# Batched norms in the query and key path of a two-layer hybrid block: copy out of PSUM by ScalarE, one reciprocal root per product

## The chip, the core and the metric

The kernel runs on one core of one Trainium2 chip. The metric is device time in microseconds (us) of one execution. Before the change it is 1564.75 us, the median of three runs (1563.94 to 1565.75). The trace comes from one further profiled execution, which took 1565.54 us; its instructions span 1563.8 us.

The engines are named as in the profile: PE (TensorE, matrix products and transposes), PEld (its weight loads), DVE (VectorE), ACT (ScalarE), POOL (GpSimd), SP (SyncE, which issues the DMAs). Each engine runs its own instructions strictly in order; they wait for each other by semaphores.

## The reference, cut to what matters

```python
for l in range(2):                                  # 512 latent tokens, 256 context tokens, width 1024
    h  = modulate(rms_norm(x,  g_mix[l]), sh1, sc1)
    hc = modulate(rms_norm(xc, g_mix[l]), csh1, csc1)
    aq, ak, av, bu, bv, cin, dq, dk, dv = split_cols(h @ w_in[l])     # and the same of hc
    # (in the last layer only keys and values are taken of hc)
    q_a = axial_rope(rms_norm(heads(aq, 4), a_q_gain[l]), rows, cols) # heads of 64
    k_a = axial_rope(rms_norm(heads(ak, 2), a_k_gain[l]), rows, cols)
    out_a = window_attention(q_a, k_a, ...)                           # + context keys + sink
    out_d = neighbourhood_attention(rms_norm(heads(dq, 4), d_q_gain[l]),
                                    rms_norm(heads(dk, 4), d_k_gain[l]), ...)
    out_b = spatial_gating(bu, bv, ...);  out_c = multiscale_pool(cin, ...)
    x = x + g1 * (concat(out_a, out_b, out_c, out_d) @ w_out[l])
    x = x + g2 * swiglu(modulate(rms_norm(x, g_ffn[l]), sh2, sc2), ...)
    # layer 0: the context tokens go the same way, with dense attention among themselves
```

What the change touches is `rms_norm(heads(...))`: every query and key head of 64 numbers is scaled by `1 / sqrt(mean(q*q) + 1e-6)`, one root per token and head.

## The kernel before

All products are float32, split into a high and a low part; one product is three matmuls (`mm3`, lines 65, 66 and 67). Tokens of the input projection lie in three tiles of 256, called 4 (the context), 0 and 2 (`tiles`, line 550). `tok_proj` (line 535) makes one tile's product in one PSUM bank: two halves of 128 tokens, eight slices of the width, three matmuls each, 48 matmuls of 256 columns.

`post_qk` (line 473) follows each such product. ACT squares the bank into an SBUF tile (L479), DVE sums each head's squares (L481), ten small DVE instructions take the reciprocal root (`rsqrt`, L100 to L109), DVE multiplies the bank by it (L484), so the bank is free after L484. Then come the gain (L486), for window attention the rotation (L495 to L498), up to four PE transposes into the one "tq" bank (L510), and the splits of that bank into high and low parts for the scores: ACT L525, L531, L532, DVE L526, L533. The next tile's transposes need that bank empty.

There are 23 such calls. In layer 0: `d_proj(0)` three, `d_proj(1)` three, `a_proj` three for keys and three for queries. In layer 1: `d_ctx` two on one bank, each `d_proj` two, `a_proj` three and two.

Neighbourhood attention of a pair of heads is `d_group`: four blocks of 128 queries (`d_pair`, line 615), in layer 0 two context blocks more (`ctx_pair`). A block does for each of its two heads: scores (PE L367, L368, four matmuls into an "sc" bank), two DVE instructions that add the bias and take the running minimum into an SBUF tile "T" (L628, L630), the exponential (ACT L359, with a row of its own for the sum), the reciprocal (DVE L361) and the scaling (DVE L362). Then PE transposes T (L337), ACT copies the transposes (L344), PE multiplies them by the values (L349, into "po"), and ACT copies that out (L354). Window attention (`a_group`) is alike.

The stages of a layer, in the order of the program: pools and values, `d_proj(0)`, `d_group(0)`, `d_proj(1)`, in layer 0 `mod_unit` (which makes modulation vectors: matmuls L154, transposes L143), `d_group(1)`, `a_proj`, `a_group(0)`, `b_proj`, `a_group(1)`; then the output projection and the feed-forward part.

That order is not the order on the engines. The framework plays the whole program through when it builds it and lets each engine take what is ready first, so products of a later stage are put between the matmuls of an attention block. What holds this back are the rings of tiles: a tag has a fixed number of buffers, handed out in the order of the program, and the user of a buffer waits for the last reader of the one before.

```python
BUFS = {"h": 8, "x": 8, "st": 8, "w": 6, "raw": 3, "mraw": 2, "T": 3, "pts": 3, "bias": 2, "row": 3, "post": 4,
        "br": 1}                                          # SBUF rings, lines 31 and 32
BANKS = {"pj": 2, "sc": 2, "tq": 1, "pt": 1, "po": 1, "md": 1}   # PSUM banks, line 33
```

So there are two "pj" banks for products, one "tq" bank, three "T" tiles, which attention alone uses, and four "post" tiles, which `post_qk` and `b_proj` use. The bias tiles of a `d_pair` (ring "bias") are made by POOL (L612).

Of the kernel before, what the change touches and what calls it, by code (L numbers as in the profile page):

```python
# [27 lines left out]
EPS = 1e-6  # L28
# [11 lines left out]
def hybrid_block(ctx: ExitStack, tc, t, out):  # L40
# [53 lines left out]

    def rsqrt(src, n, scale, eps):

        x = small.tile([128, 8], F32, tag="rx", name="rx")[:, :n]
        y = small.tile([128, 8], F32, tag="ry", name="ry")[:, :n]
        z = small.tile([128, 8], F32, tag="rz", name="rz")[:, :n]
        V.tensor_scalar(x, src, scale, eps, op0=OP.mult, op1=OP.add)  # L100
        V.tensor_scalar(y.bitcast(I32), x.bitcast(I32), -0.5, MAGIC, op0=OP.mult, op1=OP.add)
        V.tensor_mul(z, y, y)
        V.scalar_tensor_tensor(z, z, -0.5, x, op0=OP.mult, op1=OP.mult)
        V.scalar_tensor_tensor(y, z, 1.5, y, op0=OP.add, op1=OP.mult)
        V.tensor_mul(z, y, y)
        V.tensor_mul(z, z, x)
        V.tensor_scalar(x, z, 0.375, -1.25, op0=OP.mult, op1=OP.add)
        V.tensor_mul(z, z, x)
        V.scalar_tensor_tensor(y, z, 1.875, y, op0=OP.add, op1=OP.mult)  # L109
        return y  # L110
# [274 lines left out]
    for l in range(DEPTH):  # L385
# [84 lines left out]

        grid = "p (r b c) -> p b r c"

        def post_qk(ps, b, nq, nk, gain, ng, rope, Q, K, window, c0=0):

            nh = nq + nk
            p3 = ps.rearrange("p (i x) -> p i x", i=2)[:, :, c0:c0 + 64 * nh].rearrange("p i (h d) -> p i h d", d=64)
            flat = "p i h d -> p (i h) d"
            s2 = tile("post", [128, 2, nh, 64])
            S.activation(s2, p3, AF.Square)  # L479
            ss = small.tile([128, 8], F32, tag="ss", name="ss")  # L480
            V.tensor_reduce(ss[:, :2 * nh], s2.rearrange(flat), axis=AX.X, op=OP.add)  # L481
            r = rsqrt(ss[:, :2 * nh], 2 * nh, 1.0 / 64, EPS).rearrange("p (i h) -> p i h", i=2)
            n_ = tile("post", [128, 2, nh, 64])
            V.tensor_tensor(n_, p3, r.unsqueeze(3).to_broadcast([128, 2, nh, 64]), op=OP.mult)  # L484
            if ng:
                V.tensor_tensor(n_[:, :, 0:ng], n_[:, :, 0:ng],  # L486
                                gain.unsqueeze(1).unsqueeze(1).to_broadcast([128, 2, ng, 64]), op=OP.mult)
            if rope:
                rot = tile("post", [128, 2, nh, 64])
                for i in range(2):  # L490
                    nv = n_[:, i].rearrange("p h (x f c) -> p h x f c", x=2, f=2)
                    rv = rot[:, i].rearrange("p h (x f c) -> p h x f c", x=2, f=2)
                    sv = sinT[:, b + i].rearrange("p (x f c) -> p x f c", x=2, f=2)
                    for f in range(2):
                        V.tensor_tensor(rv[:, :, :, f], nv[:, :, :, 1 - f],  # L495
                                        sv[:, :, f].unsqueeze(1).to_broadcast([128, nh, 2, 16]), op=OP.mult)
                V.tensor_tensor(n_, n_, cosT[:, b:b + 2].unsqueeze(2).to_broadcast([128, 2, nh, 64]), op=OP.mult)
                V.tensor_add(n_, n_, rot)  # L498
            t0 = 128 * b

            w = window and b < 4
            pt = psum("tq")
            for j in range(nh // 2):
                for i in range(2):
                    dst = pt[:, 256 * j:256 * j + 256]
                    if w and 2 * j < nq:
                        dst = dst.rearrange("p (w i r c) -> p i r w c", w=4, i=2, r=2)[:, i]
                    else:
                        dst = dst[:, 128 * i:128 * i + 128]
                    T.transpose(dst, n_[:, i, 2 * j:2 * j + 2], ident)  # L510
            halves = [slice(64 * e, 64 * e + 64) for e in range(2)]
            for j in range(nh // 2):
                src = pt[:, 256 * j:256 * j + 256]
                if 2 * j < nq:

                    for e in range(2):
                        own, other = [Q[j][halves[x], e] for x in (e, 1 - e)]
                        if w:
                            own, other = [x[:, :SEQ].rearrange("p (w y x) -> p w y x", w=4, y=2)[:, :, b // 2]
                                          for x in (own, other)]  # L520
                            y = src[halves[e]].rearrange("p (w x) -> p w x", w=4)
                        else:
                            own, other = [x[:, t0:t0 + 256] for x in (own, other)]
                            y = src[halves[e]]
                        S.activation(own, y, AF.Copy)  # L525
# [33 lines left out]
        def d_ctx():  # L559

            w = wsplit(t["win_dk"][0], eng=G) + wsplit(t["win_dk"][1], eng=G)
            Ks = []
            ps = tok_proj(w, 4, 0, 256)
            for p in range(2):
                Ks.append(d_keys())
                post_qk(ps, 4, 0, 2, gd, 0, False, None, Ks[p], True, 128 * p)
            return Ks

        def d_proj(p, K=None):
# [1 line left out]
            bs = (0, 2) if K else tiles  # L571
            K = K or d_keys()
            Q = tile("st", [128, 2, NT], F32R)
            for bi, b in enumerate(bs):
                ps = tok_proj(w, b, 0, 256, [["pj", "sc", "pj"], ["pj", "pj", "pj"]][p][bi])
                post_qk(ps, b, 2, 2, gd, 2, False, [Q], K, True)
            return Q, K

        def d_values(pss, tag):
# [94 lines left out]
        def a_proj():  # L674
# [2 lines left out]
            K = d_keys()  # L677
            VA = tile("row", [128, 6, 128])
            w = group_units("win_a", 1)
            for b in tiles:  # L680
                ps = tok_proj(w, b, 0, 256)
                S.activation(VA[:, b:b + 2], ps.rearrange("p (i x) -> p i x", i=2)[:, :, 128:256], AF.Copy)
                post_qk(ps, b, 0, 2, gak, 2, b < 4, None, K, False)
            Q = [tile("st", [128, 2, NT], F32R) for _ in range(2)]
            w = group_units("win_a", 0)
            for b in tiles:
                if last and b == 4:
                    continue
                ps = tok_proj(w, b, 0, 256)
                post_qk(ps, b, 4, 0, gaq, 4, b < 4, Q, None, False)  # L690
            return Q, K, VA, amask


# [394 lines left out]
```

## Time and profile before

| what | value |
|---|---|
| median of three runs | 1564.75 us |
| the profiled execution | 1565.54 us, of which its instructions span 1563.8 us |
| PE | 1518.4 us busy, 97% of the span |
| DVE | 963.7 us, 62% |
| ACT | 618.1 us, 40% |
| POOL | 122.2 us, 8% |
| DMA | 104 GB/s in the mean |

How to read it: PE is the engine that is busy nearly throughout, so a microsecond counts when it makes PE stand still or makes its instructions longer. "Idle before, releaser" names the instruction whose end ended a wait. The ends of matmuls are modelled (a row of 0.28 us is followed by the next after 0.12 us), so what a matmul costs is read from the starts of successive rows. PEclk is the granted clock of TensorE, 1.00 at its upper level of 2.4 GHz; a stretch in which part of the time is at the lower level of 1.2 GHz shows a number between 0.5 and 1.

### The profile page before, as it was taken

To read this page: it belongs to the slowest core of one execution; us is meant where nothing else is said; L and a number is where in the kernel's file an instruction comes from. 1 tells how busy PE (TensorE), PEld (TensorE's weight loads), DVE (VectorE), ACT (ScalarE), POOL (GpSimd) and SP (SyncE) were. 2 spreads that over 40 slices of the span, in tenths; PEclk is the share of its full clock that TensorE was granted. 3 is DMA by queue.
4 is the path that set the end of the run, shared out by engine and by line. 5 is a ranking of instruction groups with operands and counts; after the bars stand their busy time and mean duration, and the time that the engine had idled before them with its cause. 6 is when DMAs were issued, how large, how long until landed. Compare 5 with 4: busy or idle time off the path is not lost.

```text
span 1563.8 us, 26196 instructions
## 1 busy us (share of the span) xinstructions
PE 1518.4 (97%) x10098; PEld 1336.1 (85%) x10098; DVE 963.7 (62%) x2335; ACT 618.1 (40%) x1276; POOL 122.2 (8%) x107
## 2 busy tenths in 40 slices
PE   7889999999999999999999998899999999999999
PEld 4668888788888888888888887788889998998997
DVE  4797876686485624833384467789856543454453
ACT  5546655643322112221222354457654332332331
POOL 2431000000000000000000005632000000000000
PEclk9899999999999999999999999999999999999999
DMA  8433133342243313622272231111223333223323
GB/s 309 122 115 116 48 110 129 122 139 75 88 142 113 117 62 115 222 59 64 93 248 59 78 113 55 58 55 47 81 82 102 95 84 105 90 87 102 95 82 100
DMA packets 79325, 163.39 MB, mean 104 GB/s; under 512 B 12001, under 2 KB 17761, under 8 KB 79201
## 3 DMA queue, kind: packets, MB, share of 16 engines
q1 hardware_dynamic: 79200, 161.73, 32.8%
q8 instruction: 79, 1.29, 0.3%
q14 instruction: 46, 0.37, 0.1%
HBM read 157.50 MB, written 4.19 MB: 103 GB/s over the span
## 4 chain that ended last, share of the span: by engine, by line
PE 89%; DVE 5%; ACT 1%; issue 0%; DVEq 0%; ACTq 0%
PE pj L65 9%; PE pj L66 9%; PE pj L67 9%; PE sc L66 6%; PE sc L65 6%; PE sc L67 6%; PE tq L65 3%; PE po L349 3%; PE tq L66 3%; PE tq L67 3%; PE po L65 3%; PE po L66 3%; PE po L67 3%; PE pt L66 2%; PE pt L67 2%; PE pt L65 2%
## 5 line engine op out<-in xcount | busy, mean ns | idle before, releaser
L82 ACT ACTIVATE w<-raw 128x512 fp32r<-128x512 f32 x368 | 227.5, 621 | 640.1 <-PE sc L67 159.5
L83 DVE TENSOR_TENSOR w<-raw,w 128x512 fp32r<-128x512 f32 x336 | 227.3, 679 | 244.7 <-ACT w L82 244.2
L65 PE MATMUL pj<-w,h 128*128 128x256 f32 x480 | 141.5, 295 | 12.8 <-DVE post L484 6.7
L66 PE MATMUL pj<-w,h 128*128 128x256 f32 x480 | 140.0, 292 | 2.9 <-DVE w L83 2.9
L67 PE MATMUL pj<-w,h 128*128 128x256 f32 x480 | 139.4, 291 | 0.0
L65 PE MATMUL pj<-st,w 128*128 128x258 f32 (+2 forms) x384 | 120.6, 314 | 2.5 <-ACT st L253 2.3
L66 PE MATMUL pj<-st,w 128*128 128x258 f32 (+2 forms) x384 | 120.4, 314 | 0.7 <-DVE st L254 0.7
L66 PE MATMUL sc<-st,w 128*128 128x258 f32 (+2 forms) x384 | 120.0, 313 | 0.0
L65 PE MATMUL sc<-st,w 128*128 128x258 f32 (+2 forms) x384 | 119.9, 312 | 0.0
L67 PE MATMUL pj<-st,w 128*128 128x258 f32 (+2 forms) x384 | 119.8, 313 | 0.0
L67 PE MATMUL sc<-st,w 128*128 128x258 f32 (+2 forms) x384 | 119.2, 311 | 0.0
L65 PEld LDWEIGHTS pj<-w,h 128*128 128x128 f32 x480 | 94.4, 197 | 21.1 <-issue 9.3
L83 POOL TENSOR_TENSOR w<-raw,w 128x512 fp32r<-128x512 f32 x32 | 44.2, 1398 | 742.2 <-ACT w L82 721.7
L66 PEld LDWEIGHTS pj<-w,h 128*128 128x128 f32 x480 | 94.7, 197 | 4.4 <-DVE w L83 3.1
L67 PEld LDWEIGHTS pj<-w,h 128*128 128x128 f32 x480 | 94.3, 197 | 1.3 <-issue 1.2
L65 PEld LDWEIGHTS pj<-st,w 128*128 128x128 f32 x384 | 73.1, 191 | 9.5 <-ACT st L253 3.5
L66 PEld LDWEIGHTS pj<-st,w 128*128 128x128 f32 x384 | 72.8, 190 | 5.7 <-DVE st L254 0.9
L67 PEld LDWEIGHTS pj<-st,w 128*128 128x128 f32 x384 | 72.7, 190 | 5.7 <-issue 1.7
L65 PEld LDWEIGHTS sc<-st,w 128*128 128x128 f32 x384 | 73.2, 191 | 4.6
L66 PEld LDWEIGHTS sc<-st,w 128*128 128x128 f32 x384 | 72.8, 189 | 4.4
L67 PEld LDWEIGHTS sc<-st,w 128*128 128x128 f32 x384 | 72.4, 189 | 4.2
L65 PE MATMUL po<-st,w 128*128 128x512 f32 (+1 forms) x192 | 66.5, 346 | 0.0
(304 smaller groups left out, 4125.8 us busy)
## 6 DMA issues: line engine op xcount, KB each, us to landing
mraw<-in_wmod SPq DMA_DIRECT2D x80, 512.0 KB, 3.7
raw<-in_wg SPq DMA_DIRECT2D x88, 256.0 KB, 2.6
raw<-in_wu SPq DMA_DIRECT2D x88, 256.0 KB, 2.6
raw<-in_wd SPq DMA_DIRECT2D x64, 256.0 KB, 2.7
h<-in_wslab SPq DMA_DIRECT2D x16, 512.0 KB, 7.8
raw<-in_wout SPq DMA_DIRECT2D x32, 256.0 KB, 2.6
x<-in_xt SPq DMA_DIRECT2D x16, 384.0 KB, 5.8
raw<-in_wd SPq DMA_DIRECT2D x32, 192.0 KB, 2.4
```

What stands on the lines that cost most here:

```text
L65: T.matmul(ps, ah, bh, start=start, stop=False)
L66: T.matmul(ps, ah, bl, start=False, stop=False)
L67: T.matmul(ps, al, bh, start=False, stop=stop)
L82: S.activation(w[:, 0, :n], raw, AF.Copy)
L83: eng.tensor_sub(w[:, 1, :n], raw, w[:, 0, :n].bitcast(F32))
L349: T.matmul(o[64 * hh:64 * hh + 64, :128], vs[hh][lo:hi], pts[i, hh], start=i == 0, stop=i == n - 1)
```

## The change

`post_qk` is cut in two. `qk_take` copies the bank to a "post" tile on ACT (new L477), squares the bank on ACT into a tile of ring "T" (L479), and lets DVE sum the squares (L480). `qk_takes` does this for all token tiles of a product, into one 24-column tile, and then calls `rsqrt` once. `qk_give` multiplies the SBUF copy by the roots (L493), then gain (L495), rotation (whose second tile is now in ring "T" too), transposes (L519) and splits (ACT L534, L540, L541; DVE L535, L542). `rsqrt` is called 9 times rather than 23 times. `d_ctx` squares and sums its bank once.

```diff
-        def post_qk(ps, b, nq, nk, gain, ng, rope, Q, K, window, c0=0):
+        def qk_take(ps, nh, ss):
+            p3 = ps.rearrange("p (i x) -> p i x", i=2)[:, :, :64 * nh].rearrange("p i (h d) -> p i h d", d=64)
+            n_ = tile("post", [128, 2, nh, 64])
+            S.activation(n_, p3, AF.Copy)
+            s2 = tile("T", [128, 2, nh, 64])
+            S.activation(s2, p3, AF.Square)
+            V.tensor_reduce(ss, s2.rearrange("p i h d -> p (i h) d"), axis=AX.X, op=OP.add)
+            return n_
+
+        def qk_takes(n, nh, pss):
+            ss = small.tile([128, 24], F32, tag="ss", name="ss")[:, :2 * nh * n]
+            ns = [qk_take(next(pss), nh, ss[:, 2 * nh * j:2 * nh * j + 2 * nh]) for j in range(n)]
+            r = rsqrt(ss, 2 * nh * n, 1.0 / 64, EPS).rearrange("p (n i h) -> p n i h", i=2, h=nh)
+            return [(x, r[:, j]) for j, x in enumerate(ns)]
+
+        def qk_give(n_, r, b, nq, nk, gain, ng, rope, Q, K, window):
             nh = nq + nk
-            s2 = tile("post", [128, 2, nh, 64])
-            S.activation(s2, p3, AF.Square)
-            ss = small.tile([128, 8], F32, tag="ss", name="ss")
-            V.tensor_reduce(ss[:, :2 * nh], s2.rearrange(flat), axis=AX.X, op=OP.add)
-            r = rsqrt(ss[:, :2 * nh], 2 * nh, 1.0 / 64, EPS).rearrange("p (i h) -> p i h", i=2)
-            n_ = tile("post", [128, 2, nh, 64])
-            V.tensor_tensor(n_, p3, r.unsqueeze(3).to_broadcast([128, 2, nh, 64]), op=OP.mult)
+            V.tensor_tensor(n_, n_, r.unsqueeze(3).to_broadcast([128, 2, nh, 64]), op=OP.mult)
...
             if rope:
-                rot = tile("post", [128, 2, nh, 64])
+                rot = tile("T", [128, 2, nh, 64])
...
         def d_proj(p, K=None):
...
-            for bi, b in enumerate(bs):
-                ps = tok_proj(w, b, 0, 256, [["pj", "sc", "pj"], ["pj", "pj", "pj"]][p][bi])
-                post_qk(ps, b, 2, 2, gd, 2, False, [Q], K, True)
+            tags = ["pj", "pj" if p else "sc", "pj"]
+            for b, x in zip(bs, qk_takes(len(bs), 4, (tok_proj(w, b, 0, 256, tags[i]) for i, b in enumerate(bs)))):
+                qk_give(*x, b, 2, 2, gd, 2, False, [Q], K, True)
```

What this does to the order of the instructions is shown at three places.

On PE in layer 0, about the transposes of `d_proj(0)`; before, with the products of its third tile (pj_1524) and the modulation's L154 about those of its second tile:

```order
L67 MATMUL pj_1440<-w_1432,h_692 128x256
L154 MATMUL md_1692<-mraw_1695,cact_79 32x512 x2
L154 MATMUL md_1692<-mraw_1701,cact_79 32x512 x2
L510 MATMUL tq_1007<-ident_75,post_1004 128x2x4x16 x2
L510 MATMUL tq_1007<-ident_75,post_1004 128x128 x2
L154 MATMUL md_1692<-mraw_1703,cact_79 32x512 x2
L154 MATMUL md_1692<-mraw_1709,cact_79 32x512 x2
L65 MATMUL pj_1524<-w_1417,h_635 128x256
```

After the change, at the same place (pj_1470 is the second product of `d_proj(1)`, sc_1116 the first scores of `d_group(0)`):

```order
L67 MATMUL pj_1470<-w_1407,h_692 128x256
L154 MATMUL md_1642<-mraw_1651,cact_79 32x512 x2
L519 MATMUL tq_1032<-ident_75,post_904 128x128 x4
L154 MATMUL md_1642<-mraw_1653,cact_79 32x512 x2
L154 MATMUL md_1642<-mraw_1659,cact_79 32x512 x2
L154 MATMUL md_1642<-mraw_1661,cact_79 32x512 x2
L519 MATMUL tq_1049<-ident_75,post_958 128x2x4x16 x2
L519 MATMUL tq_1049<-ident_75,post_958 128x128 x2
L154 MATMUL md_1642<-mraw_1667,cact_79 32x512 x2
L154 MATMUL md_1642<-mraw_1669,cact_79 32x512 x2
L143 MATMUL md_1677<-ident_75,mraw_1675 128x128 x4
L519 MATMUL tq_1066<-ident_75,post_1012 128x2x4x16 x2
```

The three tiles' transposes, which had products between them, follow one another with only L154 and L143 between; the products have moved ahead of all three.

On ACT in layer 0, in `d_group(0)`; before, at its first exponentials (post_1657 takes the squares of the second product of `d_proj(1)`, pj_1608):

```order
L359 ACTIVATE T_1146,sum_1150<-T_1146,m1_1147 128x448
L82 ACTIVATE w_2048<-raw_2046 128x512
L82 ACTIVATE w_2306<-raw_2304 128x512
L479 ACTIVATE post_1657<-pj_1608 128x512
L157 ACTIVATE mraw_1725<-md_1692 128x512
L82 ACTIVATE w_2311<-raw_2309 128x512
L525 ACTIVATE st_1439<-tq_1509 64x256
L359 ACTIVATE T_1160,sum_1164<-T_1160,m1_1161 128x448
```

After, at the last exponentials of the same group (L668, those of the second context block); pj_1416 and pj_1470 are the first two products of `d_proj(1)`, which were copied out by L477 ahead of the group's first exponential:

```order
L668 ACTIVATE T_1369,sum2_1370<-sc_1360,mn_1366 128x256
L668 ACTIVATE T_1369,sum2_1370<-sc_1361,mn_1366 128x256
L344 ACTIVATE pts_1314<-pt_1313 128x384
L344 ACTIVATE pts_1314<-pt_1313 64x128
L479 ACTIVATE T_1467<-pj_1416 128x512
L354 ACTIVATE x_1103<-po_1304 128x8x16
L479 ACTIVATE T_1521<-pj_1470 128x512
L344 ACTIVATE pts_1349<-pt_1348 128x512
```

The squares of the next product, which stood between the exponentials, stand behind the last of them.

On PE in layer 1, in `d_group(1)`; before, a stretch of a block (pj_11140 is a product of `a_proj`, sc scores, pt transposes, po the product with the values):

```order
L65 MATMUL pj_11140<-w_11033,h_9606 128x256
L367 MATMUL sc_10607<-st_9878,st_10355 128x256
L368 MATMUL sc_10607<-st_9875,st_10355 128x256
L337 MATMUL pt_10566<-ident_75,T_10542 128x128 x2
L337 MATMUL pt_10566<-ident_75,T_10542 64x128
L66 MATMUL pj_11140<-w_11033,h_9606 128x256
L349 MATMUL po_10309<-pts_10311,row_9744 64x128
L67 MATMUL pj_11140<-w_11033,h_9606 128x256
L349 MATMUL po_10309<-pts_10319,row_9744 64x128
```

After, the same group at its first block:

```order
L337 MATMUL pt_10425<-ident_75,T_10401 128x128 x2
L337 MATMUL pt_10425<-ident_75,T_10401 64x128
L337 MATMUL pt_10425<-ident_75,T_10401 128x128
L367 MATMUL sc_10504<-st_9701,st_10226 128x256
L368 MATMUL sc_10504<-st_9698,st_10226 128x256
L337 MATMUL md_10434<-ident_75,T_10415 128x128 x2
L337 MATMUL md_10434<-ident_75,T_10415 64x128
L337 MATMUL md_10434<-ident_75,T_10415 128x128
L349 MATMUL po_10424<-pts_10426,row_9663 64x128
L367 MATMUL sc_10518<-st_9701,st_10226 128x256
```

No product stands in the group any more until its last block; the group's own transposes, scores and value products follow each other.

## Rows read from the trace of the kernel before

**Rows 1.** The page's busy times, share of the span and instructions of each engine.

```profile
PE 1518.4 (97%) x10098; PEld 1336.1 (85%) x10098; DVE 963.7 (62%) x2335; ACT 618.1 (40%) x1276; POOL 122.2 (8%) x107
```

**Rows 2.** Busy time by stretches: PE, PEld, DVE, ACT, POOL, clock, DMA share, GB/s.

```profile
70.00:115.00 45.00, 38.16 (x268) 32.63 (x266) 42.87 (x102) 24.25 (x50) 18.51 (x15) 0.94 0.32 100
115.00:310.00 195.00, 194.32 (x1565) 162.59 (x1564) 145.69 (x510) 116.09 (x287) 12.86 (x16) 1.00 0.33 107
...
975.00:1026.00 51.00, 40.17 (x294) 38.75 (x294) 41.73 (x98) 20.49 (x44) 30.30 (x28) 0.92 0.21 65
1026.00:1165.00 139.00, 139.00 (x1099) 121.99 (x1098) 111.50 (x373) 91.19 (x222) 18.32 (x16) 1.00 0.19 60
```

**Rows 3.** Waits of PE: us in total, times, longest.

```profile
PE tq L510 <- DVE st L533: 6.7, 2, 3.5
PE pj L65 <- DVE post L484: 6.7, 3, 3.5
```

**Rows 4.** Timeline of ACT and DVE: first and last split of a tile.

```profile
121.28 0.38 ACT L525 ACTIVATE st<-tq 64x256 fp32r<-64x256 f32 x1 [3.96 <-PE tq L510]
...
125.15 0.43 DVE L533 TENSOR_TENSOR st<-tq,st 64x256 fp32r<-64x256 f32 x1 [0.15 <-ACT st L532]
```

**Rows 5.** Lines view, 70 to 310 us, L154: count, busy us, mean ns.

```profile
L154 PE MATMUL md<-mraw,cact 128*32 128x512 f32 x96 | 21.1, 638 | 0.0
```

**Rows 6.** Timeline of PE in layer 1: start, duration, instruction, idle time before.

```profile
997.49 0.38 PE L65 MATMUL pj<-w,h 128*128 128x256 f32 x1 [2.52 <-DVE post L484]
997.72 0.28 PE L66 MATMUL pj<-w,h 128*128 128x256 f32 x1
997.83 0.28 PE L67 MATMUL pj<-w,h 128*128 128x256 f32 x1
...
1003.57 0.52 PE L65 MATMUL pj<-w,h 128*128 128x256 f32 x1 [3.55 <-DVE post L484]
...
1004.11 0.41 PE L67 MATMUL pj<-w,h 128*128 128x256 f32 x1
1004.32 0.41 PE L65 MATMUL pj<-w,h 128*128 128x256 f32 x1
```

**Rows 7.** Lines view by form, 1040 to 1090 us: attention of layer 1.

```profile
L630 DVE TENSOR_SCALAR_CACHE_REDUCE T<-sc,m 128x256 f32<-128x256 f32 x14 | 6.7, 477 | 0.1
L362 DVE TENSOR_SCALAR T<-T,rs 128x512 f32<-128x512 f32 x8 | 6.1, 767 | 0.0
L359 ACT ACTIVATE T<-T,m 128x512 f32<-128x512 f32 x8 | 5.8, 719 | 3.0 <-DVE T L630 2.0 <-DVE rz L103 0.9
...
L628 DVE CUSTOM_DVE_ANT_0 T<-sc,bias 128x256 f32<-128x256 f32 x8 | 3.3, 415 | 0.0
...
L361 DVE RECIPROCAL rs<-sum 128x1 f32<-128x1 f32 x14 | 2.2, 157 | 0.4 <-ACT T L359 0.3
```

**Rows 8.** The same view, 80 to 310 us: layer 0.

```profile
L362 DVE TENSOR_SCALAR T<-T,rs 128x512 f32<-128x512 f32 x16 | 7.8, 485 | 0.1
```

**Rows 9.** Timeline of PE: value products of two successive blocks of layer 1.

```profile
1054.24 1.09 PE L349 MATMUL po<-pts,row 128*64 128x128 f32 x14
1055.26 0.66 PE L337 MATMUL md<-ident,T 128*128 128x128 f32 x4
1055.67 0.37 PE L367 MATMUL sc<-st 128*128 128x256 f32 x1
...
1060.10 1.09 PE L349 MATMUL po<-pts,row 128*64 128x128 f32 x14
```

**Rows 10.** One line by form: count, least, median and largest duration in ns.

```profile
L109 DVE SCALAR_TENSOR_TENSOR ry<-rz,ry x29: 144/165/1353, 44.1 to 1193.1; 128x8 f32<-128x8 f32 x15, 128x4 f32<-128x4 f32 x10, 128x6 f32<-128x6 f32 x4
...
L479 ACT ACTIVATE post<-pj x21: 361/588/605, 87.3 to 1076.6; 128x512 f32<-128x512 f32 x13, 128x256 f32<-128x256 f32 x8
...
L484 DVE TENSOR_TENSOR post<-pj,ry x21: 419/690/692, 95.9 to 1083.3; 128x512 f32<-128x512 f32 x13, 128x256 f32<-128x256 f32 x8
...
L486 DVE TENSOR_TENSOR post<-post,d_q_gain x10: 407/424/1506, 96.6 to 1027.1; 128x256 f32<-128x256 f32 x10
```

More of the change, by code (lines that the diff above doesn't have):

```diff
@@ L95, in rsqrt @@
     def rsqrt(src, n, scale, eps):
-        x = small.tile([128, 8], F32, tag="rx", name="rx")[:, :n]
-        y = small.tile([128, 8], F32, tag="ry", name="ry")[:, :n]
-        z = small.tile([128, 8], F32, tag="rz", name="rz")[:, :n]
+        x = small.tile([128, 24], F32, tag="rx", name="rx")[:, :n]
+        y = small.tile([128, 24], F32, tag="ry", name="ry")[:, :n]
+        z = small.tile([128, 24], F32, tag="rz", name="rz")[:, :n]
         V.tensor_scalar(x, src, scale, eps, op0=OP.mult, op1=OP.add)
@@ L471, in hybrid_block @@
         grid = "p (r b c) -> p b r c"
-        def post_qk(ps, b, nq, nk, gain, ng, rope, Q, K, window, c0=0):
-            nh = nq + nk
-            p3 = ps.rearrange("p (i x) -> p i x", i=2)[:, :, c0:c0 + 64 * nh].rearrange("p i (h d) -> p i h d", d=64)
-            flat = "p i h d -> p (i h) d"
-            s2 = tile("post", [128, 2, nh, 64])
-            S.activation(s2, p3, AF.Square)
-            ss = small.tile([128, 8], F32, tag="ss", name="ss")
-            V.tensor_reduce(ss[:, :2 * nh], s2.rearrange(flat), axis=AX.X, op=OP.add)
-            r = rsqrt(ss[:, :2 * nh], 2 * nh, 1.0 / 64, EPS).rearrange("p (i h) -> p i h", i=2)
-            n_ = tile("post", [128, 2, nh, 64])
-            V.tensor_tensor(n_, p3, r.unsqueeze(3).to_broadcast([128, 2, nh, 64]), op=OP.mult)
+        def qk_take(ps, nh, ss):
[12 more added lines that the diff above has]
+        def qk_give(n_, r, b, nq, nk, gain, ng, rope, Q, K, window):
+            nh = nq + nk
+            V.tensor_tensor(n_, n_, r.unsqueeze(3).to_broadcast([128, 2, nh, 64]), op=OP.mult)
             if ng:
@@ L561, in d_ctx @@
             w = wsplit(t["win_dk"][0], eng=G) + wsplit(t["win_dk"][1], eng=G)
-            Ks = []
-            ps = tok_proj(w, 4, 0, 256)
+            Ks = [d_keys() for _ in range(2)]
+            (n_, rn), = qk_takes(1, 4, (tok_proj(w, b, 0, 256) for b in (4,)))
             for p in range(2):
-                Ks.append(d_keys())
-                post_qk(ps, 4, 0, 2, gd, 0, False, None, Ks[p], True, 128 * p)
+                x = slice(2 * p, 2 * p + 2)
+                qk_give(n_[:, :, x], rn[:, :, x], 4, 0, 2, gd, 0, False, None, Ks[p], True)
             return Ks
@@ L679, in a_proj, with keys @@
             w = group_units("win_a", 1)
[L680 to L683, printed above, removed]
+            def keys():
+                for b in tiles:
+                    ps = tok_proj(w, b, 0, 256)
+                    S.activation(VA[:, b:b + 2], ps.rearrange("p (i x) -> p i x", i=2)[:, :, 128:256], AF.Copy)
+                    yield ps
+            for b, x in zip(tiles, qk_takes(3, 2, keys())):
+                qk_give(*x, b, 0, 2, gak, 2, b < 4, None, K, False)
             Q = [tile("st", [128, 2, NT], F32R) for _ in range(2)]
             w = group_units("win_a", 0)
[L686 to L690, printed above, removed]
+            bs = tiles[1:] if last else tiles
+            for b, x in zip(bs, qk_takes(len(bs), 4, (tok_proj(w, b, 0, 256) for b in bs))):
+                qk_give(*x, b, 4, 0, gaq, 4, b < 4, Q, None, False)
             return Q, K, VA, amask
```

## The prediction

> **What bounds the kernel now.** I read the busy times first: PE works 1518.4 of 1563.8 us [rows 1], so the kernel is as long as PE's work plus 45.4 us in which PE stands still. The change adds and removes no matmul, so its worth is the change in PE's idle time, and in the clock at which PE works. The stretches come next [rows 2]: around the first query and key products of either layer (70 to 115 us and 975 to 1026 us) PE misses 6.8 and 10.8 us, while DVE is busy for 42.87 of 45 and 41.73 of 51 us. In the attention that follows, PE is full: 194.32 of 195 us in layer 0, 139.00 of 139 us in layer 1. Last, the waits of PE [rows 3]: 6.7 us for the "tq" bank to be emptied (L533), 6.7 us for a "pj" bank to be released by L484. These 13.4 us are what an earlier release of the banks can save. Full attention stretches can only lose.
>
> **Part one, the root taken once.** 23 calls of `rsqrt` become 9: 14 x 10 small DVE instructions at 0.165 us [rows 10], 23 us of DVE. In the two DVE-bound stretches this is what stood in front of L484 and L533; I count the 13.4 us as gone. Elsewhere it lies beside a full PE and is worth nothing.
>
> **Part two, the copies.** 22 copies of at most 0.59 us on ACT (the price of L479, which reads the same bank [rows 10]), 13 us at most. ACT is busy 20 to 24 us in those two stretches of 45 and 51 [rows 2], so they are hidden; without that cover each would put 0.59 us behind a product.
>
> DVE's L493 now reads two SBUF tiles where L484 read PSUM and SBUF. L484 never took over 0.692 us; L486, which reads two SBUF tiles, took up to 1.506 against a median of 0.424 [rows 10], in a layer whose first product stretch has POOL busy 30.30 of 51 us [rows 2]. The Trainium skill (SBUF — State Buffer, "Who interferes with whom") states the rule that speaks against the change here: a VectorE instruction with two SBUF inputs contends with a GpSimd instruction that reads SBUF, one with at most one does not. The trace agrees with it. By that rule the four L493 nearest to POOL's work in layer 1 could each grow by 1.1 us (1.506 less 0.424), some 4 us more, and the time would come out near 1599; I leave it in the range, since the gaps between the instructions on POOL are as likely a place.
>
> **Part three, the squares in ring "T": the part that decides.** "T" has three buffers, handed out in program order, and attention uses them. The squares of `d_proj(1)` come after all T tiles of `d_group(0)`, those of `a_proj` after those of `d_group(1)`. So a product's bank is not released before the group ahead of it is nearly over, and with two "pj" banks PE can be two products ahead and no more. The order shows it: ACT's squares have moved from between the exponentials to behind the last, and no product is left in the groups of layer 1. What PE does there is then its own work at the pace of the chain DVE, ACT, DVE, PE, ACT, PE.
>
> PE's own work in a block: 8 scores at 0.12 us (the distance of two products' starts [rows 6]), 0.96; 8 transposes at 0.41 for four (1055.26 to 1055.67), 0.82; 16 value products at 1.02 for 14 (1054.24 to 1055.26), 1.17 [rows 9]; sum 3.0. DVE's: twice L628, L630, L361 and L362, 2 x (0.415 + 0.477 + 0.157 + 0.485) = 3.1 in layer 0, 2 x (0.415 + 0.477 + 0.157 + 0.767) = 3.6 in layer 1, where L362 is longer [rows 7, 8]. The pace of a block without products is on no row. It lies between PE's 3.0 and the 5.9 of two successive blocks with products in them (1054.24 to 1060.10 [rows 9]). I take DVE's own, the nearest row, and 0.7 for two heads' hand-overs between three engines: 3.9 and 4.3. PE idles 0.9 a block in layer 0, 1.3 in layer 1. Of four blocks I count three, as the first is in the next term.
>
> The first head of a group: after the last tile's transposes its splits must run, 4.3 us from L525 to the end of L533 [rows 4], of which the first head needs about 3.5; then a score, L628, L630, L359, L361, L362, 0.25 + 0.415 + 0.477 + 0.719 + 0.157 + 0.49 (0.77 in layer 1) = 2.5 to 2.8 [rows 7, 8], say 2.9 with hand-overs. PE has 16 scores, 1.9 us, to do in those 6.4: idle 4.5.
>
> The transposes of a product's tiles: they share one "tq" bank, so 4.3 us lie between two tiles [rows 4], less what stands between them. L154 costs 21.1 / 96 = 0.22 us [rows 5], and four L143, transposes like L337, 0.4.
>
> - Layer 0, `d_proj(0)`: between tiles six L154 (1.3), then four L154 and four L143 (1.3): 3.0 + 3.0 = 6.0. First head of `d_group(0)`: 4.5 less ten L154 among the scores, 2.2: 2.3. Its blocks have L154 between them and cost nothing.
> - Layer 0, `d_proj(1)`: 16 product matmuls (1.9) and six L154 (1.3) stand between the first two tiles, four L154 and four L143 between the next: 1.1 + 3.0 = 4.1. First head of `d_group(1)` 4.5, three blocks at 0.9 are 2.7, its context pairs 0.6 (as a block's share). Layer 0: 6.0 + 2.3 + 4.1 + 4.5 + 2.7 + 0.6 = 20.2.
> - Layer 1, `d_proj(0)`: two tiles, nothing between: 4.3. First head 4.5, three blocks at 1.3: 3.9. `d_proj(1)`: 42 product matmuls (5.0) between its tiles, nothing lost. First head 4.5, three blocks 3.9. Layer 1: 21.1.
> - `a_proj` keeps products between its tiles in both layers (43 matmuls and more, 5.2 us against 4.3): nothing. `a_group` keeps its products, as `b_proj` uses "post" and not "T": nothing.
>
> New idle time 41.3 us, less the 13.4: +27.9.
>
> **The clock.** After the gap of 3.55 us the distance of two products' starts was 0.21 us rather than 0.12 (1004.11, 1004.32): the lower level, 1.2 GHz; after the 2.52 us before 997.49 it stayed 0.11, the upper [rows 6]. The clock of the two stretches, 0.94 and 0.92 [rows 2], says that at most 0.06 x 45 + 0.08 x 51 = 6.8 us went there; I take 5 for three long gaps, 1.7 each. After the change four waits are as long: the one between tiles in layer 1 and three first heads. 4 x 1.7 less 5 is +2.
>
> **Sum.** 1565.5 (the profiled execution) + 27.9 + 2 = 1595.4. It stood 0.8 above the median of the three runs, so I forecast 1595.
>
> **Rivals.**
> - *PE turns slow in the unfilled groups, or the chain is slower than I take it.* At the pace of 5.9 [rows 9] the blocks cost 2.0 and 1.6 more: 3 x 2.0 + 6 x 1.6, with some 3 in `d_group(0)`, +19: 1613. At the lower clock a block's own work is 6.0 rather than 3.0, 2.1 and 1.7 over the pace, with the score and transpose work of the first heads +24: 1619. For it: three engines in one ring of three tiles. Against the clock's part: around the gap of 2.52 us PE stayed at the upper level [rows 6]. The Trainium skill (TensorE: Matmul & The Clock Gate, "A second HAM failure mode: psum-queue depth-cycling") describes just this, frequent short idles that make the clock swing between its levels; the trace here shows both outcomes, so it stays a rival.
> - *The relief wins: faster.* The banks' early copy takes the 13.4 us and the 5 of the clock, and DVE, freed of 23 us, empties "tq" in step with the transposes and feeds the heads so far ahead that the groups cost little. It decides where the new idle time stays under 18: at 8 it gives 1564.75 - 18.4 + 8 = 1554. For it: DVE is nearly full in both early stretches [rows 2]. Against it: the 4.3 us chain [rows 4] holds no root, so it is not shortened, and the moved products can't come back.
> - *Near no change:* PE's other idle time shrinks by about what is new, because blocks run at PE's own 3.0 and the first heads hide their splits: six blocks at 1.3 and three at 0.9 (10.5) and half of the 18 us of first heads and context go; 1595 - 10.5 - 9 = 1576, and with part of the tiles' gaps, 1565.
>
> **How the numbers follow.** Forecast and its neighbourhood (1581 to 1607) 0.56; slow chain or clock (1607 to 1625) 0.18; slower, but less than forecast (1568 to 1581), 0.08; within 0.2%, about what a measurement of this kernel can tell from no change (1562 to 1568), 0.06; faster 0.12. That makes slower 0.82. The range 1562 to 1620 leaves out the relief and the end of the slow case. The likeliest case alone spans 1581 to 1607.
>
> **What would show it.** In the profile after: DVE some 23 us less busy, ACT some 12 more; no wait of a product for a bank in the two early stretches; waits of L519 for L542 of up to 4 us, several of them; waits of the first L337 of a group for L362; PE idle time of some 73 us in all (45.4 + 27.9), the new idle time between 90 and 310 us and between 1000 and 1090 us, none beyond. The prediction is wrong if products fill the groups after all, if PE idles under 55 us, or if the feed-forward part changes.

## The result, and the profile after

The changed kernel takes 1616.18 us (median of four runs, 1613.69 to 1617.36) against 1564.36 us before (the median once the profiled execution is counted in): 1.0325 of before, 95% interval 1.0313 to 1.0337. It is slower by 52 us; forecast were 30. The profiled execution took 1617.36 us, its instructions span 1615.6.

The page's busy times of the kernel after, which answer to [rows 1]:

```profile
PE 1543.5 (96%) x10098; PEld 1345.9 (83%) x10098; DVE 939.2 (58%) x2194; ACT 631.4 (39%) x1297; POOL 122.7 (8%) x107
```

The span is 51.8 us longer. PE's idle time went from 45.4 to 72.1 us (1615.6 - 1543.5), +26.7; the forecast had +27.9. But PE is also *busy* for 25.1 us more with the same 10098 matmuls, for which the forecast had 2. DVE has 24.5 us less to do, and the kernel is slower all the same.

The stretches of the kernel after, which answer to [rows 2] (columns as there):

```profile
70.00:115.00 45.00, 42.28 (x305) 38.28 (x304) 35.56 (x77) 22.32 (x43) 18.83 (x16) 0.96 0.27 89
115.00:200.00 85.00, 69.96 (x432) 41.42 (x432) 36.24 (x118) 38.35 (x98) 7.34 (x11) 0.89 0.50 154
200.00:330.00 130.00, 120.32 (x949) 107.45 (x949) 97.17 (x309) 76.56 (x182) 2.99 (x2) 0.95 0.18 57
...
1000.00:1060.00 60.00, 44.62 (x304) 41.04 (x304) 45.18 (x93) 31.45 (x63) 34.23 (x29) 0.88 0.22 68
1060.00:1110.00 50.00, 47.82 (x362) 39.91 (x363) 30.78 (x116) 30.26 (x87) 5.34 (x8) 0.90 0.06 16
```

The first stretch got better, as expected of the earlier release: PE 42.28 of 45 us rather than 38.16, DVE 35.56 rather than 42.87. The attention behind it, where PE was full at clock 1.00, now has idle time and a clock of 0.89 and 0.95. PE's waits of the kernel after, which answer to [rows 3]:

```profile
PE md L154 <- DMA mraw<-in_wmod: 9.4, 5, 3.5
...
PE tq L519 <- DVE st L542: 7.5, 4, 4.8
...
PE pj L65 <- DVE st L754: 5.8, 1, 5.8
PE sc L367 <- DVE st L535: 5.0, 5, 1.8
PE tq L519 <- DVE post L507: 3.5, 1, 3.5
```

The waits of a product for L484 are gone, as forecast. Transposes wait for the "tq" bank, first scores for the splits (L535), as forecast. Three lines were not: L154, which the forecast had as filler between the transposes and which itself waits 9.4 us for its weights, and L754 and L507, of which below.

Where in the program the time went is read from two landmarks: the first pool instruction of layer 1 (L788, L800 after) and the last residual of the feed-forward part (L898, L910 after). The one-line view of the kernel before, then after (duration least, median, largest in ns; first and last start):

```profile
L788 DVE TENSOR_TENSOR st<-pj,row x4: 404/407/677, 72.4 to 972.7; 128x256 f32<-128x256 f32 x3, 128x512 f32<-128x512 f32 x1
...
L898 DVE SCALAR_TENSOR_TENSOR x<-pj,mod,x x24: 470/748/751, 328.3 to 1531.5; 128x512 f32<-128x512 f32 x16, 128x256 f32<-128x256 f32 x8
```

```profile
L800 DVE TENSOR_TENSOR st<-pj,row x4: 406/410/679, 73.0 to 1010.0; 128x256 f32<-128x256 f32 x3, 128x512 f32<-128x512 f32 x1
...
L910 DVE SCALAR_TENSOR_TENSOR x<-pj,mod,x x24: 474/750/751, 370.5 to 1583.3; 128x512 f32<-128x512 f32 x16, 128x256 f32<-128x256 f32 x8
```

Layer 0 ends at 1010.0 rather than 972.7, 37.3 us later; layer 1 takes 573.3 rather than 558.8 from there, 14.5 more. The same two starts in every experiment are in the table at the end of the next section.

### The profile page after: what moved, and what is told of

The parts are those of the page before. It is cut to its first block, busy times and chain, and to the rows that moved or that the text cites. A ratio compares the mean times of both kernels' runs of the same rounds, so it can differ in the third digit from the quotient of the medians.

```text
span 1615.6 us, 26084 instructions
## 1 busy us (share of the span) xinstructions
PE 1543.5 (96%) x10098; PEld 1345.9 (83%) x10098; DVE 939.2 (58%) x2194; ACT 631.4 (39%) x1297; POOL 122.7 (8%) x107
## 4 chain that ended last, share of the span: by engine, by line
PE 83%; DVE 5%; issue 4%; DMA 2%; ACT 2%; POOL 1%; ACTq 0%; POOLq 0%; DVEq 0%
PE pj L66 8%; PE pj L65 8%; PE pj L67 8%; PE sc L65 6%; PE sc L66 6%; PE sc L67 6%; PE tq L65 3%; PE tq L66 3%; PE tq L67 3%; PE po L66 3%; PE po L65 3%; PE po L67 3%; PE po L349 3%; PE pt L66 2%; PE pt L65 2%
```

## The experiments

"Of before" is the ratio of the runs to runs of the kernel before on the same chip, with its 95% interval.

**One word: squares in ring "T", nothing else (e4).**

```diff
 # in the kernel before
-            s2 = tile("post", [128, 2, nh, 64])
+            s2 = tile("T", [128, 2, nh, 64])
```

> The kernel before with one word changed: the squares lie in ring T instead of post; no copy, no batch. Theory ring: this alone makes 1595 to 1620. Rival batch: within 5 us of 1564.

1614.99 us, 1.0321 of before (1.0305 to 1.0336), as slow as the whole change. PE of this kernel at the borders of `d_group(0)` in layer 1 (start, duration, idle before and its releaser):

```profile
1047.21 1.09 PE L510 MATMUL tq<-ident,post 128*128 128x128 f32 x4 [5.35 <-DVE st L533]
1049.22 0.58 PE L367 MATMUL sc<-st 128*128 128x256 f32 x1 [0.92 <-DVE st L526]
...
1071.60 0.58 PE L65 MATMUL pj<-w,h 128*128 128x256 f32 x1 [2.00 <-DVE post L484]
```

Transposes wait for the "tq" bank and the first scores for the splits, as in the changed kernel, with no batch and no copy. Between 1049 and 1071 us stands the group alone, and the next product waits for the bank that L484 can only release once its square has had a T tile. How many product matmuls stand in this group is read from the instructions on "pj" alone (start and end, length, PE busy and how many, clock), in the kernel before, in this one and in the changed kernel:

```profile
1030.00:1060.00 30.00, 20.30 (x142) 1.00 0.14 40
```

```profile
1049.20:1071.50 22.30, 0.00 (x0) 0.81 0.03 7
```

```profile
1055.20:1072.70 17.50, 0.00 (x0) 0.79 0.03 9
```

**The whole change, but squares out of "T" (e1).**

```diff
-            s2 = tile("T", [128, 2, nh, 64])
-            S.activation(s2, p3, AF.Square)
-            V.tensor_reduce(ss, s2.rearrange("p i h d -> p (i h) d"), axis=AX.X, op=OP.add)
+            S.activation(p3, p3, AF.Square)
+            V.tensor_reduce(ss.rearrange("p (i h) -> p i h", i=2), p3, axis=AX.X, op=OP.add)
```

> The changed kernel, but ACT squares the bank in place (after the copy) and DVE sums the squares out of PSUM, so no square lies in ring T any more; the batched root, the copies and one rotation tile in T stay. Theory ring (squares in T hold the banks until attention's T tiles are through, which empties the attention groups of products): most of the 52 us come back, 1555 to 1575, and products stand in the groups of layer 1. Rival batch (one root per product sends all tiles through one tq bank in a row, whatever ring holds the squares): 1600 or more.

1564.93 us, 0.9993 of before (0.9983 to 1.0002): all 52 us are back, and PE is busy for 1514.1 us with the same matmuls, at a clock of 0.989. Products stand in that group again (as above):

```profile
1035.00:1060.00 25.00, 13.10 (x88) 1.00 0.19 57
```

The two together settle it: squares in ring "T" are needed for the loss, and they are enough. A larger ring "T" was not run.

**One root per tile again (e2), and the copies alone (e3).**

```diff
 # e2: of the kernel after
-            ns = [qk_take(next(pss), nh, ss[:, 2 * nh * j:2 * nh * j + 2 * nh]) for j in range(n)]
-            r = rsqrt(ss, 2 * nh * n, 1.0 / 64, EPS).rearrange("p (n i h) -> p n i h", i=2, h=nh)
-            return [(x, r[:, j]) for j, x in enumerate(ns)]
+            for j in range(n):
+                ss = small.tile([128, 24], F32, tag="ss", name="ss")[:, :2 * nh]
+                x = qk_take(next(pss), nh, ss)
+                yield x, rsqrt(ss, 2 * nh, 1.0 / 64, EPS).rearrange("p (i h) -> p i h", i=2)
 # e3: e2, and squares and rotation in ring "post"
-            s2 = tile("T", [128, 2, nh, 64])
+            s2 = tile("post", [128, 2, nh, 64])
-                rot = tile("T", [128, 2, nh, 64])
+                rot = tile("post", [128, 2, nh, 64])
```

> The changed kernel with one root per token tile again (23 calls of rsqrt), each tile given on before the next product is taken; the copies and the squares in ring T stay. Theory ring: the groups stay empty, 1600 to 1625. Rival batch: back to 1560 to 1575.

1601.83 us, 1.0232 of before (1.0217 to 1.0247): still slow, so the batch is not the cause; but it is 14 us better than the whole change, all of it in layer 0 (992.1 against 1010.0). (`rsqrt` is called 22 times in it, not 23, as `d_ctx` keeps its single sum; so too in e3, e8 and e9.) With the squares in T the batch makes it worse.

> One root per tile, squares and rotation in ring post as before the change; of the change only ACT's copy out of PSUM is left (and the single sum of d_ctx). Theory ring: 1555 to 1570, the wait of a product for L484 gone (6.7 us) or replaced by one on the ring post. Rival (the copies crowd ACT): 1575 or more.

1560.92 us, 0.9973 of before (0.9961 to 0.9985): ACT's copy, with the single sum of `d_ctx`, is a gain of 4 us. PE waits 1.5 us in all for "tq" in this run, and no longer for a bank that a root holds, though there are as many roots as before but one.

**The modulation's loads (e5, with its control e6).** After the result I took the 9.4 us of waits for weights as the reason for layer 0.

```diff
             for kk in range(4):
-                raws = [load_raw(t["wmod"][mods["l"], u, 2 * kk + i], tag) for i in range(2)]
+                if kk == 0 or mods["l"] or u not in (2, 3, 4):
+                    raws = [load_raw(t["wmod"][mods["l"], u, 2 * kk + i], tag) for i in range(2)]
```

> The changed kernel with three quarters of the modulation's weight loads in layer 0's mod_unit left out (each unit loads its first pair of slabs and uses it four times), so L154 hardly waits for a DMA. In the changed kernel PE waits 9.4 us for these loads, in places where only L154 stands between two tiles' transposes or before the first scores. Theory paced by loads: that, and the lower clock beside it, is why layer 0 lost 37 us and not the 16 predicted; the time falls by 10 to 22 us against the changed kernel's 1616. Rival (the tq bank would hold PE in the same places anyway): it falls by less than 5.

> The control: the kernel before with the same loads left out. There L154 stands among products and waits 1.8 us for loads. Both theories: within 4 us of the kernel before.

1609.39 us, 1.0286 of before (1.0271 to 1.0302), 6.8 us less than the changed kernel; the control 1557.79 us, 0.9954 (0.9939 to 0.9969), 7 us less than before. Both expectations of e5 missed (6.8 lies between 5 and 10), and so did that of the control, which was to stay within 4 us. But the loads are worth the same in both kernels, so the theory falls. The waits of PE in e5 show what took their place, the rival named in the expectation (L520 and L543 are L519 and L542 there):

```profile
PE tq L520 <- DVE st L543: 15.4, 6, 5.0
...
PE md L155 <- DMA mraw<-in_wmod: 2.7, 3, 1.4
```

The wait for loads fell by 6.7 us and that for the "tq" bank rose by 7.9, nearly all of it at the transposes of `d_proj(1)` in layer 0, where PE now waits 3.20 and 4.39 us for the bank: the bank sets the pace there, and the loads only came last.

**A second bank for the second tile of `d_proj` in layer 1 (e7).**

```diff
-            pt = psum("tq")
+            pt = psum("md" if last and nq == 2 and b == 2 else "tq")
```

> The changed kernel, but in layer 1 the second tile of either d_proj is transposed into the bank md, so it needn't wait until tq is empty. In the changed kernel PE waits 4.84 us there, and works at the lower clock for about 10 us behind. Theory clock: the time falls by more than the wait, 6 to 9 us. Theory idle time alone: by 3 to 5 us. Rival (the splits themselves, in order on ACT and DVE, decide when the first scores start): by less than 2 us.

1609.74 us, 1.0285 of before (1.0269 to 1.03), 6.4 us less than the changed kernel; layer 1 takes 565.3 us rather than 573.3, 8.0 less. PE of the changed kernel there, then of e7 (start, duration, idle before and its releaser):

```profile
1053.26 1.09 PE L519 MATMUL tq<-ident,post 128*128 128x128 f32 x4 [4.84 <-DVE st L542]
1055.26 0.58 PE L367 MATMUL sc<-st 128*128 128x256 f32 x1 [0.92 <-DVE st L535]
...
1058.18 0.53 PE L367 MATMUL sc<-st 128*128 128x192 f32 x1 [0.27 <-ACT st L541]
```

```profile
1050.12 0.38 PE L367 MATMUL sc<-st 128*128 128x256 f32 x1 [1.73 <-DVE st L535]
1051.84 0.38 PE L367 MATMUL sc<-st 128*128 128x256 f32 x1 [1.23 <-DVE st L535]
1052.83 0.35 PE L367 MATMUL sc<-st 128*128 128x192 f32 x1 [0.49 <-ACT st L541]
1054.09 0.53 PE L367 MATMUL sc<-st 128*128 128x192 f32 x1 [0.28 <-ACT st L541]
```

The gaps sum to 6.0 us and to 3.7, 2.3 less. In the changed kernel the first scores behind the long gap take 0.58 and 0.53 us, at the lower level; in e7 they take 0.38, at the upper, until 1053, and then 0.53 too. PE's busy time in the whole kernel is 1538.1 rather than 1543.5. That looks as if the long wait cost more than its length, but the edit touches two places, and the 8.0 us come in two parts. Stretches of the changed kernel, then of e7: from the start of layer 1 to the first product behind `d_group(0)`, and from there to the same product behind the blocks of `d_group(1)` (columns as above):

```profile
1010.00:1072.80 62.80, 53.45 (x382) 0.88 0.18 55
1072.80:1111.00 38.20, 36.02 (x274) 0.91 0.06 17
```

```profile
1010.80:1069.30 58.50, 52.70 (x381) 0.90 0.20 59
1069.30:1103.70 34.40, 32.46 (x274) 1.00 0.06 19
```

Around the long wait the kernel gained 4.3 us, of which 3.6 are idle time: there the wait cost little more than its length. Around `d_proj(1)` and `d_group(1)` the same 274 matmuls take 3.8 us less, of which only 0.2 are idle time: the clock is 1.00 rather than 0.91. In the changed kernel the first scores of this group start behind the last product, with gaps of 0.2 to 1.0 us before and between them, 2.2 in sum; in e7 the first of them stand among products, and the gaps sum to 1.6. So the time fell as the theory of the clock has it, but not at the place that it named.

**One root per tile in `a_proj` alone (e12).**

```diff
-            for b, x in zip(tiles, qk_takes(3, 2, keys())):
+            for b, x in zip(tiles, qk_each(3, 2, keys())):
...
-            for b, x in zip(bs, qk_takes(len(bs), 4, (tok_proj(w, b, 0, 256) for b in bs))):
+            for b, x in zip(bs, qk_each(len(bs), 4, (tok_proj(w, b, 0, 256) for b in bs))):
 # qk_each: for j in range(n): yield from qk_takes(1, nh, pss)
```

> The changed kernel, but only d_ctx and d_proj take one root for all tiles; a_proj takes one per tile again (squares and rotation stay in ring T). In the changed kernel all tiles of an a_proj product are multiplied, gained and rotated in one run of DVE, some 12 us, and b_proj's DVE instructions and the first scores of a_group wait behind it: PE idles 5.8 us in layer 0 (for L754) and 3.5 + 1.8 us in layer 1 (for L507 and L535). Theory bunching: these go, with the lower clock behind them; the time falls by 10 to 20 us against the changed kernel's 1616. Rival (ring T, which the rotation is in, holds a_proj whatever the batch): within 5 us of 1616.

1606.57 us, 1.0263 of before (1.0247 to 1.0278): 9.6 us less, just short of the 10 to 20. The wait for L754 is gone from layer 0 and most of that for L507 from layer 1, where however only 1.4 us came of it; 9.0 came in layer 0. The changed kernel's DVE shows what was meant by one run (start, duration):

```profile
253.69 1.90 DVE L493 TENSOR_TENSOR post<-post,ry 128x512 f32<-128x512 f32 x3
255.51 1.89 DVE L495 TENSOR_TENSOR post<-post,a_q_gain 128x512 f32<-128x512 f32 x3
257.43 0.69 DVE L752 SCALAR_TENSOR_TENSOR post<-post,pj 128x512 f32<-128x512 f32 x1
258.03 1.70 DVE L504 TENSOR_TENSOR T<-post,sinT 128x128 f32<-128x128 f32 x8
...
262.11 0.68 DVE L752 SCALAR_TENSOR_TENSOR post<-post,pj 128x512 f32<-128x512 f32 x1
262.71 0.69 DVE L507 TENSOR_TENSOR post<-post,T 128x512 f32<-128x512 f32 x1
...
264.59 1.29 DVE L754 SCALAR_TENSOR_TENSOR st<-post,pj 128x512 f32<-128x512 f32 x2
```

All tiles' multiplications, gains and rotations stand together, and L752 and L754, which release `b_proj`'s banks, are queued in and behind them. PE at that place:

```profile
265.42 0.55 PE L65 MATMUL pj<-w,h 128*128 128x256 f32 x1 [5.75 <-DVE st L754]
```

**The batch without ring T (e8, e10), and more room for the copies (e9).** e8 is e1 with e2's loop. e10 and e9 are:

```diff
 # e10: of the kernel after
-        "br": 1}
+        "br": 1, "sq": 1}
-            s2 = tile("T", [128, 2, nh, 64])
+            s2 = tile("sq", [128, 2, nh, 64])
 # and rx, ry, rz, ss with bufs=2
 # e9: of e3
-... "post": 4,
+... "post": 5,
 # and rx, ry, rz, ss of 8 columns
```

> As the run with the squares in the bank (e1: 0.9993 of before), but with one root per token tile. The difference between the two is the batched root alone, free of ring T. If the batch costs by sending the tiles through tq in a row: 3 to 6 us faster than e1, 1559 to 1562. If the 140 DVE instructions saved are worth something: slower than e1.

1573.28 us, 1.0056 of before (1.004 to 1.0073): 8 us *slower* than e1. Layer 0 is the same (978.0 against 977.9), layer 1 takes 561.4 rather than 551.7. So with the squares in the bank, which holds it until DVE has summed them, one root for all tiles is worth about 10 us in layer 1. (The loop also hands each tile on before the next product is taken, so what is compared is the batch with its order.) Layer 0 also limits what e12 showed: PE waits 5.2 us in e1 for the same release behind the batch (L753 there), e8 is without that wait, and the layer is no shorter for it.

> The changed kernel with the squares in an SBUF tile of their own (a ring of one buffer; the small tiles of the root in rings of two to make room), batch, copies and rotation in T kept. Against the squares in the bank (e1, 0.9993 of before), a bank is released 0.7 us or more earlier. Theory: 1555 to 1564, between e3 and e1 or better. Rival (one buffer for squares makes ACT wait for DVE's sum): 1565 or more.

1573.44 us, 1.0053 of before (1.004 to 1.0065): the rival holds in so far as it is slower. PE waits 9.8 us for "tq" and 5.8 for L754 in it, and only once, 0.47 us, for the square's tile. I can't say that the single buffer is why; that stays open.

> The run with copies only (e3, 0.9973 of before) with five buffers in ring post rather than four, small tiles of 8 columns again. If that ring holds the banks in e3: 2 to 4 us faster than e3, 1556 to 1559. If not: within 2 us of e3's 1561.

1563.09 us, 0.9986 of before (0.9977 to 0.9995), 0.13% more than e3 (2.2 us; expected were 2 to 4 less, or within 2): a fifth buffer brings no gain, so the ring "post" does not hold the banks in e3.

**The better half of each (e11).** `s2` is the bank itself and the root is batched in layer 1; in layer 0 squares and rotation lie in "post", with one root per tile.

```diff
 # of e1
-            S.activation(p3, p3, AF.Square)
+            s2 = p3 if last else tile("post", [128, 2, nh, 64])
+            S.activation(s2, p3, AF.Square)
...
-                rot = tile("T", [128, 2, nh, 64])
+                rot = tile("T" if last else "post", [128, 2, nh, 64])
 # qk_takes: groups of m = n if last else 1 tiles per root
```

> Layer 0 as in the run with copies only (e3: layer 0 2.5 us shorter than before), layer 1 as in the run with the squares in the bank and the batched root (e1: layer 1 7 us shorter than before). If the layers' gains add: 1564 - 2.5 - 7, 1552 to 1558. If e1's layer 1 owed its time to what its layer 0 left behind: 1560 or more.

1557.45 us, 0.9951 of before (0.9939 to 0.9964): 0.5% faster than before and 3.6% faster than the changed kernel, where the sum of the layers' gains said. It is the best of all these kernels that do the whole work. PE of it, 37.6 us idle:

```profile
PE 1516.6 (98%) x10098; PEld 1333.5 (86%) x10098; DVE 948.0 (61%) x2274; ACT 629.3 (40%) x1297; POOL 119.8 (8%) x107
```

The layers of every kernel, from its profiled execution (first pool instruction of layer 1; from there to the last residual in a "pj" bank), and PE's idle and busy time:

| kernel | layer 0 ends | layer 1 | PE idle | PE busy |
|---|---|---|---|---|
| before | 972.7 | 558.8 | 45.4 | 1518.4 |
| after | 1010.0 | 573.3 | 72.1 | 1543.5 |
| e4, T alone | 997.8 | 582.3 | 73.0 | 1539.4 |
| e2, T and copies | 992.1 | 573.7 | 63.7 | 1534.4 |
| e12, batch not in a_proj | 1001.0 | 571.9 | 69.4 | 1535.8 |
| e7, second bank | 1010.8 | 565.3 | 70.3 | 1538.1 |
| e5, fewer loads | 998.4 | 575.3 | 78.7 | 1527.5 |
| e6, before with fewer loads | 964.3 | 558.9 | 42.4 | 1513.4 |
| e1, squares in the bank | 977.9 | 551.7 | 47.8 | 1514.1 |
| e8, e1 with root per tile | 978.0 | 561.4 | 51.2 | 1520.5 |
| e10, squares in own ring | 987.3 | 553.2 | 54.5 | 1518.3 |
| e3, copies alone | 970.2 | 556.3 | 40.7 | 1518.1 |
| e9, e3 with five "post" | 970.9 | 558.1 | 43.1 | 1518.2 |
| e11, by layer | 969.3 | 552.6 | 37.6 | 1516.6 |

## Why the prediction was right, and where it was not

**The mechanism was right.** The squares in ring "T" empty the attention groups of products, and that alone makes the kernel slower: e4 and e1 show it from both sides. The waits for L484 went, as said. The size was not: forecast were 1595 us and 1581 to 1607 as the likeliest case, and the 1616 lie in the range only because it was drawn wide enough for most of a rival that was given 0.18.

**What the relief was put down to was wrong.** Part one counts 13.4 us of early waits as gone because the root is taken once. In e3 no product waits behind a root any more and "tq" costs 1.5 us, with 22 roots: so the copy is enough for it. The batch itself, with the squares in "T", costs 14 us (e2). Nor is 0.165 us, the median, the price of the root's small instructions everywhere: [rows 10] has an L109 of 1.353 us, and L104 and L108 of the same root took up to 1.449 and 1.668 in the kernel before, each of these while an instruction of POOL ran.

**The idle time was right in sum, by luck, not in its places.** Against the terms of the sum, from PE's gaps in the kernel after:

| place | forecast | measured |
|---|---|---|
| layer 0, `d_proj(0)` to the first head | 6.0 + 2.3 | 8.1 |
| layer 0, `d_proj(1)` to the first head | 4.1 + 4.5 | 6.7 |
| layer 0, blocks and context of `d_group(1)` | 2.7 + 0.6 | 2.0 |
| layer 1, `d_proj(0)` to the first head | 4.3 + 4.5 | 6.0 |
| layer 1, first head of `d_group(1)` | 4.5 | 2.2 |
| layer 1, blocks of both groups | 3.9 + 3.9 | 0 |
| `a_proj`, `b_proj` and the first head of `a_group` | 0 | 5.8 + 3.5 + 1.8 |

The 36.1 us measured at these places come near the 41.3 forecast because 11.1 that nobody forecast stand against 16.3 that did not come, 7.8 of them the blocks' of layer 1. Two signs failed with them: no L337 waits for L362, and 5.3 us of new idle time lie beyond 1090 us. Three figures of the working are slightly off by its own terms (3.1 + 0.7 is 3.8, not 3.9; the first heads and context pairs sum to 16.4, not 18; the largest L479 is 0.605, not 0.59); none of them moves a forecast by 1 us.

The pace of a block without products, the cost that no row of before showed, was taken too slow. Value products of three successive blocks in layer 1 after:

```profile
1064.99 1.39 PE L349 MATMUL po<-pts,row 128*64 128x128 f32 x14
...
1068.78 1.09 PE L349 MATMUL po<-pts,row 128*64 128x128 f32 x14
...
1071.37 1.09 PE L349 MATMUL po<-pts,row 128*64 128x128 f32 x14
```

3.8 and 2.6 us (the second without scores of its own, which had run ahead), 3.2 in the mean, where 4.3 was forecast and PE's own work was reckoned at 3.0: PE has no gap there. So the empty groups themselves cost next to nothing; the price is paid at their borders, where products used to stand between the tiles' transposes and ahead of the first scores.

**"`a_proj` keeps products between its tiles: nothing" failed.** The products were there, but the step looked only at the "tq" bank. Batching the root also gathers all tiles' DVE work into one run, and the next product's release is queued behind it on DVE. e12 takes that away and gives back 9.6 us in the changed kernel; e1 and e8, above, show no such gain with the squares in the bank.

**The clock, +2 in the sum, is the term that was mis-sized.** It was priced at four long gaps of 1.7 us. Stretches of the kernel after (start and end, length, PE busy, clock):

```profile
1050.00:1060.00 10.00, 5.36 (x15) 0.62 0.23 73
189.00:206.00 17.00, 13.65 (x42) 0.50 0.31 93
260.00:270.00 10.00, 4.58 (x21) 0.70 0.00 0
1090.00:1097.00 7.00, 6.48 (x24) 0.51 0.00 1
```

Taken in stretches of 2 us, PE's busy time times what the clock lacks of 1.00 sums to 3.4 us in layer 0's mixing stages before (70 to 328 us) and 4.9 in layer 1's (950 to 1165); after, to 13.9 (70 to 365) and 11.7 (987 to 1217). That is +17.3 rather than +2. The long waits were more than four, with those at L154, L754 and L507; and behind them stood scores and L154, with further pauses, not dense products as before: from 189 to 206 us the clock stayed at the lower level, where behind [rows 6]'s gap of 3.55 us it had recovered within about 3.5 (the clock of the kernel before is 0.66 from 1003 to 1008 us). That the sparse work kept it low is read from these places; the nearest thing to a test of it is e7's second stretch, where products stood among the scores and the clock stayed at 1.00. The other 8 of PE's 25.1 us of busy time I can't assign; PE's ends are modelled, and pauses between rows count as busy. By line most of the 25.1 lies with the scores, L367 (before, then after) and L368 (41.5 us before, 47.6 after), and with L154, which [rows 5] had at 21.1:

```profile
L367 PE MATMUL sc<-st 128*128 128x256 f32 (+2 forms) x160 | 45.0, 301 | 0.1
```

```profile
L367 PE MATMUL sc<-st 128*128 128x256 f32 (+2 forms) x160 | 54.2, 353 | 6.3 <-DVE st L535 5.0 <-ACT st L541 1.1
L154 PE MATMUL md<-mraw,cact 128*32 128x512 f32 x96 | 28.0, 687 | 10.4 <-DMA mraw<-in_wmod 9.4 <-DVE st L535 1.0
```

The rival with the clock named 1619 for PE at the lower level *within* the blocks. The time came out near it, but its mechanism only in part: the first heads' scores did run at the lower level, as it has them, but the blocks ran at the upper level once under way (the scores behind 1062.7 us take 0.28 us again), and the loss lies behind the gaps:

```profile
1059.73 0.42 PE L368 MATMUL sc<-st 128*128 128x256 f32 x1
...
1062.86 0.28 PE L368 MATMUL sc<-st 128*128 128x256 f32 x1
```

What the Trainium skill says in TensorE: Matmul & The Clock Gate ("A second HAM failure mode: psum-queue depth-cycling"), that short idles make the clock swing, was weighed as part of the rival that was given 0.18. The trace after agrees with it: the clock fell behind single gaps of 3.5 us and more, and at 1090 us among gaps of 0.2 to 1.0 us, 2.2 in sum; in e7 the scores behind gaps of 1.73 and 1.23 us stayed at the upper level at first.

The rule of the Trainium skill on two SBUF inputs (SBUF — State Buffer, "Who interferes with whom") had been weighed for L493. Its line after (least, median, largest in ns):

```profile
L493 DVE TENSOR_TENSOR post<-post,ry x23: 418/684/1079, 109.8 to 1132.8; 128x512 f32<-128x512 f32 x15, 128x256 f32<-128x256 f32 x8
```

L484 never took over 692 ns; two of the 23 L493 took longer, 1030 and 1079, one behind the other, while POOL made bias tiles out of SBUF (L621, 1040.56 to 1042.84 us):

```profile
1041.36 2.03 DVE L493 TENSOR_TENSOR post<-post,ry 128x512 f32<-128x512 f32 x2
```

So the rule is borne out by two of 23, at 0.35 to 0.4 us each, far from the 4 us that it might have cost. No run isolates it. Its second half, that one SBUF input does not contend, the page states only outside the 2-port modes, and the trace before has such an input held up: L107 of the root, which reads one SBUF tile, took 1.361 us beside POOL's L796, 0.171 in the median; in which mode it ran, no row shows.

## What to carry to other kernels

When a tile moves to another ring, ask whose tiles stand before it in program order: a ring shared with another stage ties a producer's bank to the users that stand before it. Look for it in the order first: the stretches that lost their filler here paid at their borders, not inside. And a batch that saves instructions gathers the remaining ones into one run on an in-order engine: name what is queued behind that run, and who waits for it. Whether the wait costs time depends on the rest: here it did with the squares in "T", and not with the squares in the bank.

## What the runs showed of the hardware

A stage can lose more by TensorE's clock than by idle time: around `d_group(1)` of layer 1 the same 274 matmuls took 38.2 us at a granted clock of 0.91 (kernel after) and 34.4 at 1.00 (e7), and only 0.2 us of the difference is idle time. Around the long wait of 4.84 us it was the other way: 4.3 us came back there in e7, and 3.6 of them were idle time. The lower level lasted longest, from 189 to 206 us of the kernel after, where scores and L154, which waited for its weights, stood behind the gap.
